# Dividing a top-256 threshold search and its weight subtractions differently between ScalarE, VectorE and GpSimd

## The chip, the cores and the metric

The kernel is one launch on one core of one Trainium2 chip. The core has TensorE (PE) for matrix products, VectorE (DVE), ScalarE (ACT) and GpSimd (POOL) for everything else, and SyncE (SP), which here only starts DMAs. Each engine runs its own list of instructions strictly in order; an instruction whose data or buffer is not there yet holds up everything behind it on its engine. The metric is the time of one execution in device microseconds, lower is better, as the median of three runs.

## The reference, cut to what matters

The reference is one step of a two-layer trunk, for a prompt of 1024 tokens and for eight sample rows of one token each, with a model width of 1024. Layer 0 is a state-space and convolution layer and is not touched. Layer 1 is sparse attention: cheap index scores pick 256 keys for every query, and attention runs over these keys alone.

```python
def index_scores(qi, wi, ki):
    s = jnp.einsum('bthd,bsd->bths', qi, ki, preferred_element_type=jnp.float32) * IDX_DIM ** -0.5
    return jnp.einsum('bths,bth->bts', jax.nn.relu(s), wi.astype(jnp.float32) * IDX_HEADS ** -0.5)

def dsa_attend(q, qi, wi, q_pos, ki_all, gather_kv, topk):
    scores = index_scores(qi, wi, ki_all)
    key_pos = jnp.arange(ki_all.shape[1])
    admissible = key_pos[None, :] <= q_pos[:, None]
    scores = jnp.where(admissible[None], scores, -jnp.inf)
    _, idx = lax.top_k(scores, topk)
    ...
    p = jax.nn.softmax(logits, axis=-1)
    return jnp.einsum('btgrk,btkgd->btgrd', p.astype(v_sel.dtype), v_sel)

def odd_out(x, o, z, w_out, ln_g, ln_b):
    out = (o.reshape(b, l, ATTN_WIDTH) * jax.nn.silu(z)) @ w_out
    return layer_norm(ALPHA * x + out, ln_g, ln_b)
```

Here `q, k, v, qi, ki, wi, z` are slices of one product `x @ w_in`: query, key, value, the three index projections, and the gate.

## The kernel before

The 1024 prompt tokens and the eight sample tokens are one activation of 1032 columns, which layer 1 takes in three chunks of 344 (`CH`). Weights come in tiles of 128 output rows. Each product is made of three matmuls so that it keeps float32 precision: weights and activations are split into a high part, which is the value cast to the matmul's type, and a low part, which is the rest (L131 to L133: high by high, high weight by low activation, low weight by high activation). One weight tile goes through `load_w` and twice through `load_half` (a half is 128x512): a DMA fills `wst`, ScalarE casts it to `whi` (L107), and one engine subtracts to give `wlo` (L108). That engine is VectorE unless the caller passes another. There are three buffers each of `wst`, `whi` and `wlo`.

Layer 1 runs these loops on TensorE: the index projections; the index scores of query blocks 7 to 2 (`SCORE_ROWS`, a block is 128 queries and block tb sees 128(tb+1) keys); eight query tiles (QQ); two key tiles (KK); eight gate tiles (ZZ). Each chunk of a gate tile is evacuated from PSUM by ScalarE (`ev`, L1097). The attention of the eight blocks and the output projection follow. Blocks 0 and 1 have no more than 256 keys and need no search.

The samples' keys are in paged caches. GpSimd starts one indirect DMA per page group (`gather`, L843): 32 of index keys (`in_ckidx`, into an eight-slot buffer that is a tile of pool `q`; L980 multiplies them) and 64 of keys (`in_ck`, eight behind each gate tile, into three buffers; L1077 multiplies them, and a gather of a later tile waits until that has read the buffer).

The 256th largest score of every row is found bit by bit: a round counts the scores at or above a candidate and keeps or drops the candidate's bit. Two methods share the blocks:

- `topk_signs` counts on ScalarE, with the sum of signs (L1137, 32 rounds). Search `a` takes the blocks of `ACT_ROWS` (here 4 and 3: 640 and 512 wide) and search `s` the sample rows (8x1025). After the counts of a round (`jka`, `jks`), VectorE makes three small instructions (L1139, L1121, L1123), and only then can the next round's count start.
- `topk_halves` counts on VectorE. Search `d` takes `DVE_ROWS` (here 7, 6, 5, 2). A copy of each score's upper 16 bits (`UP`, L962) is searched for 16 rounds (`jkd`, L1148). One more count says how many scores are above; then `low` is made of the lower 16 bits (L1164, L1165) in tiles of pool `q`, and searched for 16 more rounds. A row of `bl` costs one count per round.

`masks` turns thresholds into additive masks on VectorE: one count, for `a` and `s` two (L1190), and per block five wide instructions (L1214 to L1218; L1215 is a running sum). The buffers of this stage are closed behind the masks, and the attention's first instruction on VectorE, L1288, which adds the mask to the logits of L1287, stands behind those of `d` and `a`.

The order of the work on each engine is not written in the code: a scheduler places each instruction by its own model of the engines when the program is built. A change in one loop can therefore move instructions of every other.

## Time and profile before

| | |
|---|---|
| runs before | 1779.60, 1783.72 and 1786.36 us, median 1783.72 us |
| the profiled execution | 1771.31 us |
| its span | 1769.5 us |
| mean granted TensorE clock | 0.971 |
| PE busy | 1646.9 us |
| DVE busy | 1076.5 us |
| ACT busy | 782.1 us |
| POOL busy | 495.5 us |
| first count of search `d` | 1037.4 us from the span's start |
| last upper-half count of `d` / last lower-half count | 1184.7 / 1290.2 us |
| first attention instruction on VectorE (L1288) | 1334.51 us |

The profile is of one execution, and instants are counted from its span's start. "Busy" counts an engine's own instructions; a busy engine is not the bound as such. What an engine waited for is inferred from semaphores. TensorE's granted clock is a share of full speed. The stage of the change is from about 990 us, where the first scores are made, to 1334.5 us, where attention begins. The profile gives line numbers of the kernel before; in the kernel after, everything behind L1121 is up to seven lines lower.

### The profile page before, as it was taken

To read this page: it belongs to the slowest core of one execution; us is meant where nothing else is said; L and a number is where in the kernel's file an instruction comes from. 1 tells how busy PE (TensorE), PEld (TensorE's weight loads), DVE (VectorE), ACT (ScalarE), POOL (GpSimd) and SP (SyncE) were. 2 spreads that over 40 slices of the span, in tenths; PEclk is the share of its full clock that TensorE was granted. 3 is DMA by queue.
4 is the path that set the end of the run, shared out by engine and by line. 5 is a ranking of instruction groups with operands and counts; after the bars stand their busy time and mean duration, and the time that the engine had idled before them with its cause. 6 is when DMAs were issued, how large, how long until landed. Compare 5 with 4: busy or idle time off the path is not lost.

```text
span 1769.5 us, 28572 instructions
## 1 busy us (share of the span) xinstructions
PE 1646.9 (93%) x10654; PEld 1467.2 (83%) x10654; DVE 1076.5 (61%) x2632; ACT 782.1 (44%) x1626; POOL 495.5 (28%) x507
## 2 busy tenths in 40 slices
PE   8999999989999999997999999798898997789996
PEld 8999999989999988996898999588795665456674
DVE  4232341551557787757566479799998755355574
ACT  4111111552445554536334355357755653346563
POOL 5242331001212242224224002601555224432120
PEclk9999999999999999998999999899998998899999
DMA  7343343344111264424422213423436333343351
GB/s 241 94 134 109 117 115 96 128 162 170 45 36 56 85 195 149 141 88 131 110 67 87 71 65 102 134 98 110 139 117 196 69 69 102 79 104 81 84 134 47
DMA packets 161836, 192.76 MB, mean 109 GB/s; under 512 B 24144, under 2 KB 122824, under 8 KB 161440
## 3 DMA queue, kind: packets, MB, share of 16 engines
q1 hardware_dynamic: 151920, 166.23, 31.7%
q0 software_dynamic: 8480, 23.31, 4.8%
q8 instruction: 84, 1.38, 0.4%
q10 hardware_dynamic: 1296, 1.38, 0.2%
q14 instruction: 56, 0.46, 0.1%
HBM read 134.73 MB, written 56.14 MB: 108 GB/s over the span
## 4 chain that ended last, share of the span: by engine, by line
PE 76%; DVE 15%; issue 3%; another core or an unknown queue 2%; DMA 2%; ACT 2%; POOL 1%; SPq 0%; DVEq 0%; ACTq 0%; POOLq 0%
PE pp L131 12%; PE pp L133 12%; PE pp L132 12%; PE po L1375 4%; DVE jkd L1148 4%; PE pt L323 4%; PE pv L1323 4%; PE lg L1287 4%; PE tr L1314 3%; PE pt L133 2%; PE pt L132 2%; PE pt L131 2%; PE pt L574 2%; DVE P L1288 1%
## 5 line engine op out<-in xcount | busy, mean ns | idle before, releaser
L131 PE MATMUL pp<-act,whi 128*128 128x344 f32 x1088 | 351.3, 324 | 9.6 <-ACT act L231 8.1
L133 PE MATMUL pp<-act,wlo 128*128 128x344 f32 x1088 | 351.9, 325 | 4.8 <-DVE wlo L108 4.8
L132 PE MATMUL pp<-act,whi 128*128 128x344 f32 x1088 | 351.3, 323 | 0.7 <-POOL act L673 0.6
L131 PEld LDWEIGHTS pp<-act,whi 128*128 128x128 f32 x1088 | 205.5, 189 | 12.2 <-ACT act L231 8.1
L133 PEld LDWEIGHTS pp<-act,wlo 128*128 128x128 f32 x1088 | 205.6, 189 | 6.8 <-DVE wlo L108 5.1
L132 PEld LDWEIGHTS pp<-act,whi 128*128 128x128 f32 x1088 | 205.6, 189 | 3.2 <-issue 1.0
L108 DVE TENSOR_TENSOR wlo<-wst,whi 128x512 fp32r<-128x512 f32 x104 | 72.7, 701 | 161.7 <-ACT whi L107 158.7
L107 ACT CAST whi<-wst 128x512 fp32r<-128x512 f32 x148 | 91.0, 618 | 173.2 <-PE pp L132 58.7
L131 PE MATMUL pp<-yh,whi 128*128 128x344 f32 x408 | 135.1, 331 | 9.0 <-issue 5.0
L133 PE MATMUL pp<-yh,wlo 128*128 128x344 f32 x408 | 133.9, 328 | 6.4 <-issue 3.7
L318 POOL TENSOR_TENSOR cft<-cw,own 128x640 f32<-128x640 f32 x64 | 86.0, 1379 | 165.8 <-PE pt L323 154.7
L1288 DVE CUSTOM_DVE_ANT_0 P<-lg,w 128x512 f32<-128x512 f32 (+3 forms) x144 | 83.1, 597 | 81.0 <-PE lg L1287 41.4
L1287 PE MATMUL lg<-w,Q 128*128 128x512 f32 (+3 forms) x384 | 107.9, 385 | 13.7 <-DVE nmx L1288 13.5
L843 POOL DMA_INDIRECT q<-in_ck,idx x64 | 68.4, 1069 | 117.3 <-PE pt L1077 83.5
L108 POOL TENSOR_TENSOR wlo<-wst,whi 128x512 fp32r<-128x512 f32 x44 | 58.1, 1324 | 150.6 <-ACT whi L107 130.5
L1314 PE MATMUL tr<-cst,P 128*128 128x128 f32 x576 | 89.1, 287 | 5.4 <-issue 3.9
L1287 PEld LDWEIGHTS lg<-w,Q 128*128 128x128 f32 x384 | 65.2, 198 | 34.5 <-DVE nmx L1288 21.8
L1314 PEld LDWEIGHTS tr<-cst,P 128*128 128x128 f32 x576 | 67.0, 145 | 32.2 <-issue 23.4
L1292 ACT ACTIVATE P<-P,mx 128x1024 f32<-128x1024 f32 (+3 forms) x64 | 63.3, 989 | 68.6 <-DVE mx L1291 56.6
L1323 PE MATMUL pv<-ph,V 128*64 128x256 f32 (+1 forms) x640 | 85.2, 381 | 8.9 <-ACT ph L1319 4.2
L131 PEld LDWEIGHTS pp<-yh,whi 128*128 128x128 f32 x408 | 78.4, 192 | 17.9 <-issue 11.0
L133 PEld LDWEIGHTS pp<-yh,wlo 128*128 128x128 f32 x408 | 78.3, 192 | 9.1 <-issue 4.9
(568 smaller groups left out, 4028.7 us busy)
## 6 DMA issues: line engine op xcount, KB each, us to landing
wst<-in_W SPq DMA_DIRECT2D x148, 256.0 KB
Q<-dq SPq DMA_DIRECT2D x64, 256.0 KB
dq<-ev SPq DMA_DIRECT2D x48, 172.0 KB
xst<-in_xT SPq DMA_DIRECT2D x8, 516.0 KB
dzb<-ob SPq DMA_DIRECT2D x24, 172.0 KB
uv<-dzb SPq DMA_DIRECT2D x8, 516.0 KB
dza<-ob SPq DMA_DIRECT2D x24, 172.0 KB
dyb<-uv SPq DMA_DIRECT2D x8, 516.0 KB
```

The costliest lines, as they stand in the source:

```text
L107: nc.scalar.copy(hi, st)
L108: (eng or nc.vector).tensor_tensor(lo, st, hi.bitcast(F32), op=ALU.subtract)
L131: nc.tensor.matmul(out, wh, ah, start=(start and kt == 0), stop=False)
L132: nc.tensor.matmul(out, wh, al, start=False, stop=False)
L133: nc.tensor.matmul(out, wl, ah, start=False, stop=(stop and kt == 7))
L318: nc.gpsimd.tensor_tensor(wt.rearrange("q d (c p) -> q d c p", p=PH), cw[:, g, : NBT - 1].rearrange("q (d p) -> q d p", p=PH).unsqueeze(2) ...
L323: nc.tensor.matmul(p[:, j, :], wt[:, d, :], up[:, g, 4 - d : 4 - d + BL], start=(d == 0), stop=(d == NSH - 1))
L1148: nc.vector.tensor_scalar(jk, col, c, 0.0, op0=op, op1=ALU.add, accum_out=cnt)
L1287: mm = nc.tensor.matmul(lg, Q[:, 4 * a + r, :], KT[g][:, s0 : s0 + m], start=(a == 0), stop=(a == 1))
L1288: nc.vector.tensor_tensor_reduce(out=P[:, s0 : s0 + m], in0=lg, in1=M[tb][:, s0 : s0 + m], scale=-0.125, scalar=BIG, op0=ALU.add, op1=ALU. ...
L1314: nc.tensor.transpose(p[:, a, r * 128 : r * 128 + 128], Ps[r][:, (sb + a) * 128 : (sb + a) * 128 + 128], k.ident)
L1323: nc.tensor.matmul(pv[64 * u : 64 * u + 64, 256 * pr + c0 : 256 * pr + c1], V[:, sb + a, g * 64 : g * 64 + 64], ph[:, a, c0:c1], start=(sb ...
```

## The change

Three things are changed, all in layer 1.

1. `SCORE_ROWS` is now 7, 6, 5, 4, 3, 2. Block 2 moves from search `d` (VectorE) to search `a` (ScalarE). A round of `a` now has three counts, one of `d` three in place of four. The `UP` copies stand behind block 5's scores.
2. The query, key and gate weights are loaded with `eng=nc.gpsimd`: 18 tiles, 36 subtractions L108 go from VectorE to GpSimd.
3. In search `d`, the update of the candidate for bits 30 to 16 is one instruction in place of two. The comparison yields 0 or the bit in its place, and one instruction flips that bit and sets the next one to be tried.

```diff
-SCORE_ROWS = (7, 6, 5, 2, 3, 4)
-ACT_ROWS = (4, 3)
-DVE_ROWS = (7, 6, 5, 2)
+SCORE_ROWS = (7, 6, 5, 4, 3, 2)
+ACT_ROWS = (4, 3, 2)
+DVE_ROWS = (7, 6, 5)
...
-        w = load_w(k, A["W"][QQ + i])
+        w = load_w(k, A["W"][QQ + i], eng=nc.gpsimd)
...
-        w = load_w(k, A["W"][KK + i])
+        w = load_w(k, A["W"][KK + i], eng=nc.gpsimd)
...
-        w = load_w(k, A["W"][ZZ + i])
+        w = load_w(k, A["W"][ZZ + i], eng=nc.gpsimd)
...
-    def search(name, R_, cols, count, above, last):
+    def search(name, R_, cols, count, above, last, placed=False):
...
-            above(no, cnt)
+            above(no, cnt, bit)
             new = k.t(tk, [R_, n], U32, "cand" + name, 2)
-            if bit == 31:
-
-                nc.vector.tensor_scalar(new.bitcast(I32), no, -1.0, None, op0=ALU.mult)
+            flip = 1 << (bit - 1) if bit > last else 0
+            if bit < 31 and placed:
+                nc.vector.scalar_tensor_tensor(new, no, flip, cand, op0=ALU.bitwise_xor, op1=ALU.bitwise_xor)
             else:
-                nc.vector.scalar_tensor_tensor(new, no, bit, cand, op0=ALU.logical_shift_left, op1=ALU.bitwise_xor)
-            if bit > last:
-                nc.vector.tensor_scalar(new, new, 1 << (bit - 1), None, op0=ALU.bitwise_xor)
+                if bit == 31:
+
+                    nc.vector.tensor_scalar(new.bitcast(I32), no, -1.0, None, op0=ALU.mult)
+                else:
+                    nc.vector.scalar_tensor_tensor(new, no, bit, cand, op0=ALU.logical_shift_left, op1=ALU.bitwise_xor)
+                if flip:
+                    nc.vector.tensor_scalar(new, new, flip, None, op0=ALU.bitwise_xor)
             cand = new
         return cand
...
-        cand = search(name, 128, UP, count, lambda no, cnt: nc.vector.tensor_scalar(no, cnt, float(TOPK), None, op0=ALU.is_lt), 16)
+        def above(no, cnt, bit):
+            nc.vector.tensor_scalar(no, cnt, float(TOPK), float(1 << bit) if bit < 31 else 1.0, op0=ALU.is_lt, op1=ALU.mult)
+
+        cand = search(name, 128, UP, count, above, 16, placed=True)
```

With other engines and other lengths, the scheduler orders the stage anew. Three places show it. In the rows, a line, an operation, and the tile written `<-` those read are given.

The first place is VectorE between the last counts of search `d`'s upper halves (`jkd` from `topd`) and its lower halves (`q<-S`, L1164). `noa`, `canda` are search `a`, `nos` is search `s`. Before:

```order
L1148 TENSOR_SCALAR jkd_12875,k2d_12870<-w_9633,topd_12868 128x896
L1161 TENSOR_SCALAR sgnd_12871<-sgnd_12871 128x4
L1139 TENSOR_TENSOR noa_12445<-cnta_12444,lima_12319 128x2
L1148 TENSOR_SCALAR jkd_12877,k2d_12870<-w_9634,topd_12868 128x768
L1164 TENSOR_SCALAR q_12885<-S_9635,sgnd_12871,offd_12872 128x1024
L1164 TENSOR_SCALAR q_12885<-S_9635,sgnd_12871,offd_12872 128x896
L1121 SCALAR_TENSOR_TENSOR canda_12451<-noa_12445,canda_12441 128x2
L1164 TENSOR_SCALAR q_12886<-S_9635,sgnd_12871,offd_12872 128x768
```

And now (L1171 is the lower half, L1143, L1125 and L1127 are a round's three small instructions):

```order
L1152 TENSOR_SCALAR jkd_12895,k2d_12888<-w_9634,topd_12886 128x768
L1143 TENSOR_TENSOR noa_12409<-cnta_12408,lima_12318 128x3
L1164 TENSOR_SCALAR k2d_12888<-k2d_12888 128x3
L1125 SCALAR_TENSOR_TENSOR canda_12417<-noa_12409,canda_12405 128x3
L1127 TENSOR_SCALAR canda_12417<-canda_12417 128x3
...
L1143 TENSOR_TENSOR noa_12445<-cnta_12444,lima_12318 128x3
L1125 SCALAR_TENSOR_TENSOR canda_12453<-noa_12445,canda_12441 128x3
L1127 TENSOR_SCALAR canda_12453<-canda_12453 128x3
L1171 TENSOR_SCALAR q_12901<-S_9635,sgnd_12889,offd_12890 128x1024
L1171 TENSOR_SCALAR q_12901<-S_9635,sgnd_12889,offd_12890 128x896
```

In place of one round of search `a`, four stand in a row ahead of the lower halves (the two left out at "..." read like those shown), and the subtractions `wlo` are gone from there.

The second place is ScalarE at the end of the search, around the last counts of `a` (`jka`) and the evacuations of the gate tiles (`ev`). Before:

```order
L1097 ACTIVATE ev_11988<-pp_11963 128x344
L1137 ACTIVATE jks_13355,cnts_13353<-Ss_9636,cands_13350 8x1025
L1137 ACTIVATE jka_12636,cnta_12634<-S_9635,canda_12631 128x640
L1137 ACTIVATE jka_12638,cnta_12634<-S_9635,canda_12631 128x512
L1097 ACTIVATE ev_12016<-pt_11991 128x344
L1137 ACTIVATE jks_13363,cnts_13361<-Ss_9636,cands_13358 8x1025
L107 CAST whi_12079<-wst_12077 128x512
L107 CAST whi_12193<-wst_12191 128x512
L1097 ACTIVATE ev_12044<-pp_12019 128x344
L1137 ACTIVATE jks_13371,cnts_13369<-Ss_9636,cands_13366 8x1025
L1097 ACTIVATE ev_12108<-pt_12083 128x344
L1137 ACTIVATE jks_13379,cnts_13377<-Ss_9636,cands_13374 8x1025
```

And now, at the last two rounds of `a`:

```order
L1141 ACTIVATE jka_12678,cnta_12672<-S_9635,canda_12669 128x384
L1141 ACTIVATE jka_12686,cnta_12684<-S_9635,canda_12681 128x640
L1141 ACTIVATE jka_12688,cnta_12684<-S_9635,canda_12681 128x512
L1097 ACTIVATE ev_12135<-pp_12110 128x344
L1141 ACTIVATE jka_12690,cnta_12684<-S_9635,canda_12681 128x384
L107 CAST whi_12198<-wst_12196 128x512
L1141 ACTIVATE jka_12698,cnta_12696<-S_9635,canda_12693 128x640
L1141 ACTIVATE jka_12700,cnta_12696<-S_9635,canda_12693 128x512
L1097 ACTIVATE ev_12163<-pt_12138 128x344
L1141 ACTIVATE jka_12702,cnta_12696<-S_9635,canda_12693 128x384
L1101 COPY ki_11337<-pt_10237 128x512
L1097 ACTIVATE ev_12227<-pp_12202 128x344
```

Before, the last count of `a` had eight of the gate stage's 24 evacuations behind it, and counts of `s` between them; now it has three behind it, and one evacuation stands inside each of its last rounds.

The third place is GpSimd in the gate tiles. Before, only the gathers of `in_ck` stood there, eight for a tile. Now, around one tile's subtractions:

```order
L843 DMA q_11340<-in_ck,idx_8869 128x256
L108 TENSOR_TENSOR wlo_11719<-wst_11716,whi_11718 128x512
L843 DMA q_11339<-in_ck,idx_8869 128x256
...
L843 DMA q_11340<-in_ck,idx_8869 128x256
L108 TENSOR_TENSOR wlo_11833<-wst_11830,whi_11832 128x512
L843 DMA q_11339<-in_ck,idx_8869 128x256
...
L843 DMA q_11339<-in_ck,idx_8869 128x256
L108 TENSOR_TENSOR wlo_11839<-wst_11836,whi_11838 128x512
L843 DMA q_11338<-in_ck,idx_8869 128x256
```

Each gate tile now has two subtractions among its eight gathers, on the same engine and in order with them; up to four gathers stand between the two.

More of the change, by code (lines that the diff above doesn't have):

```diff
@@ L1137, in count @@
             nc.scalar.activation(jk, s, AF.Sign, bias=c, scale=-1.0, accum_out=cnt)
-        return search(name, R_, bl, count, lambda no, cnt: nc.vector.tensor_tensor(no, cnt, lim, op=ALU.is_gt), 0)
+        return search(name, R_, bl, count, lambda no, cnt, bit: nc.vector.tensor_tensor(no, cnt, lim, op=ALU.is_gt), 0)
     def topk_halves(name, bl):
```

## The prediction

> **What bounds the kernel now.** I read the page first, for the engines and the chain that ended last.
>
> ```profile
> PE 1646.9 (93%) x10654; PEld 1467.2 (83%) x10654; DVE 1076.5 (61%) x2632; ACT 782.1 (44%) x1626; POOL 495.5 (28%) x507
> PE 76%; DVE 15%; issue 3%; another core or an unknown queue 2%; DMA 2%; ACT 2%; POOL 1%; SPq 0%; DVEq 0%; ACTq 0%; POOLq 0%
> ```
>
> TensorE is busy nearly throughout and carries three quarters of the chain; VectorE carries 15%. So a change on the other engines counts only where the chain leaves TensorE. The second view, the windows (stretch, its length, then busy time and instructions of PE, PEld, DVE, ACT, POOL, granted clock, DMA share, GB/s), finds that place.
>
> ```profile
> 1100.00:1150.00 50.00, 39.62 (x202) 31.00 (x202) 40.25 (x119) 18.18 (x43) 31.59 (x33) 0.86 0.49 138
> 1150.00:1200.00 50.00, 47.63 (x277) 41.50 (x276) 49.21 (x151) 28.93 (x68) 3.81 (x4) 1.00 0.32 107
> 1200.00:1250.00 50.00, 42.84 (x293) 38.95 (x292) 49.03 (x164) 36.32 (x79) 16.14 (x16) 0.97 0.38 116
> 1250.00:1300.00 50.00, 43.60 (x332) 40.86 (x332) 49.42 (x173) 37.11 (x80) 22.80 (x23) 0.97 0.40 124
> ```
>
> From 1150 to 1300 VectorE is busy 49 of every 50 us, TensorE 134.1 of 150. ScalarE and GpSimd have room: 102.4 and 42.8 of 150. VectorE is the full queue of this stage. What ends the stage stands in the chain of waits from 1250 on (start, length, engine, tile, line), of which these pieces are the last before attention.
>
> ```profile
> 1320.90 0.89 DVE eq L1190 x2
> 1333.30 1.28 DVE eq L1190 x2
> 1334.58 0.60 DVE P L1288
> ```
>
> The masks of search `a` run from 1320.9 to 1333.3 (12.4 us), after those of `d`, and one count of `s` follows; then L1288 starts attention. That alone would make VectorE's chain the bound. The timeline shows the other clock.
>
> ```profile
> 1298.87 0.73 ACT L1137 ACTIVATE jka<-S,canda 128x512 bf16<-128x512 f32 x1
> 1318.46 0.43 ACT L1097 ACTIVATE ev<-pt 128x344 f32<-128x344 f32 x1
> 1320.42 1.15 ACT L1137 ACTIVATE jks<-Ss,cands 8x1025 bf16<-8x1025 f32 x1 [0.79 <-DVE cands L1123]
> 1329.23 0.46 ACT L1097 ACTIVATE ev<-pp 128x344 f32<-128x344 f32 x1 [3.37 <-PE pp L133]
> ```
>
> ```profile
> 1330.08 1.20 PE L1287 MATMUL lg<-w,Q 128*128 128x512 f32 x4
> 1335.24 3.24 PE L1287 MATMUL lg<-w,Q 128*128 128x512 f32 x6 [3.96 <-DVE nmx L1288]
> ```
>
> The last count of `a` (first row) ended at 1299.6, 21 us before its masks could start: ScalarE was early, VectorE late. But TensorE's last gate chunk was evacuated at 1329.2 (fourth row), and its first logits stood at 1331. TensorE waited 4 us for the masks and no more. **Both chains end within 4 us of each other**, so a shorter VectorE queue is worth at most those 4 us unless TensorE's gate tiles end earlier too.
>
> **The change part by part.** All sums are for the instant of L1288, 1334.5 in the profiled execution (1771.31 us, 0.7% below the median of the runs, 1783.72; I add the difference to the median).
>
> What leaves VectorE ahead of the end of `d`'s masks (groups from 1036 to 1335: busy us, mean ns, idle before):
>
> ```profile
> L108 DVE TENSOR_TENSOR wlo<-wst,whi 128x512 fp32r<-128x512 f32 x33 | 22.5, 683 | 2.8 <-issue 2.4 <-DMA dz<-ev 0.4
> L1148 DVE TENSOR_SCALAR_CACHE_REDUCE jkd<-w,candd 128x384 bf16<-128x384 bf16 x16 | 9.7, 607 | 0.1
> L1148 DVE TENSOR_SCALAR_CACHE_REDUCE jkd<-q,testd 128x384 bf16<-128x384 uint16 x16 | 9.6, 602 | 0.0
> L1123 DVE TENSOR_SCALAR candd<-candd 128x4 uint32<-128x4 uint32 x15 | 2.7, 178 | 0.3
> L1139 DVE TENSOR_TENSOR noa<-cnta,lima 128x2 uint32<-128x2 f32 x32 | 4.8, 149 | 0.0
> ```
>
> ```profile
> 1290.82 0.68 DVE L108 TENSOR_TENSOR wlo<-wst,whi 128x512 fp32r<-128x512 f32 x1
> 1291.42 0.17 DVE L1173 TENSOR_TENSOR ged<-cntd,k2d 128x4 f32<-128x4 f32 x1
> 1318.21 0.96 DVE L1215 TENSOR_TENSOR_SCAN cum<-eq 128x384 f32<-128x384 f32 x1
> 1319.20 0.62 DVE L1216 SCALAR_TENSOR_TENSOR eq<-cum,needd,eq 128x384 f32<-128x384 f32 x1
> ```
>
> Block 2 costs 16 counts of 607 ns and 16 of 602: 19.3 us. One more count in the search and one in the masks are 1.2, its five wide mask instructions, two of which are shown, about 3 (an estimate from these two), its copy and low halves about 1: together 24. A subtraction holds the queue for 0.60 us, as the start of the next instruction shows; 33 of them are 20. The 15 second bit updates of 178 ns, each 0.15 by start to start, are 2.3. Sum: 46 us, on a queue that is full; it comes off nearly whole.
>
> What leaves the stretch without leaving the path: when the masks of `d` are done, eight rounds of `a` and eleven of `s` are still to come in the new order (before, almost none). Their 57 small instructions, of up to 0.15 us each, are 8.5 us, of which I take 6, since in a full queue starts stand closer than durations (0.60 against 0.68 above). They go to the tail.
>
> What is added: four rounds of `a` stand in a row ahead of the lower halves, with nothing between them to do, so VectorE waits there for ScalarE three times. ScalarE's durations:
>
> ```profile
> L1137 ACT ACTIVATE jks<-Ss,cands 8x1025 bf16<-8x1025 f32 x32 | 36.8, 1150 | 24.8 <-DVE cands L1123 13.2 <-issue 6.6 <-DVE canda L1121 4.5
> L1137 ACT ACTIVATE jka<-S,canda 128x640 bf16<-128x640 f32 x32 | 26.3, 822 | 25.9 <-DVE canda L1123 17.2 <-DVE nos L1139 4.7 <-DVE jkd L1148 2.5
> L1137 ACT ACTIVATE jka<-S,canda 128x512 bf16<-128x512 f32 x32 | 23.0, 718 | 0.4
> L107 ACT CAST whi<-wst 128x512 fp32r<-128x512 f32 x33 | 19.9, 609 | 3.6 <-PE pt L980 2.9 <-PE pp L132 0.5
> L1097 ACT ACTIVATE ev<-pt 128x344 f32<-128x344 f32 x12 | 5.3, 446 | 8.9 <-PE pt L133 3.3 <-PE pp L133 3.3 <-remote 2.3
> ```
>
> A count of 384 is estimated at 0.61 us, on the line through 512 (718 ns) and 640 (822). A round of `a` is then 2.15 us on ScalarE, and about 0.8 for VectorE's three instructions and the way back: the row of `jks` at 1320.42 above shows 0.79 idle on `cands`. Three rounds of 2.95, less the instructions already counted, are 8 us. It is nothing if ScalarE ran ahead, and 12 if casts and evacuations stand between; I take 8.
>
> The subtractions on GpSimd cost VectorE something too where both read their operands at once. No row shows L108 of GpSimd against a score row of VectorE; the nearest pair is from layer 0:
>
> ```profile
> 669.55 0.51 DVE L658 TENSOR_TENSOR gz<-gz,gz 128x344 f32<-128x344 f32 x1
> 670.45 2.52 DVE L658 TENSOR_TENSOR gz<-gz,gz 128x344 f32<-128x344 f32 x1
> 670.22 2.37 POOL L673 TENSOR_TENSOR act<-big,act 128x1032 fp32r<-128x1032 f32 x1 [7.00 <-ACT act L672]
> ```
>
> The same subtraction-like instruction took 0.51 us alone and 2.52 us beside GpSimd's, and ended 0.4 us after it. Of VectorE's instructions with two full operands the score updates are the main ones, and they lie with the query subtractions. If ten of the 36 meet one and hold it for half of GpSimd's 1.32 us (row below), VectorE loses 6 us, part of it in slack; I take 3. Ends: 0, and 24 if all 36 meet one. The Trainium skill, "SBUF — State Buffer", section "Who interferes with whom", says that a VectorE instruction with two SBUF inputs and a GpSimd instruction that reads SBUF exclude each other for a whole instruction, and that one with at most one SBUF input is free. By this rule of the Trainium skill each of the ten could be held for all of GpSimd's 1.32 us, 13 us in place of 3, and the sum would be 1796. The layer 0 pair agrees with it (2.52 us against 0.51).
>
> So `d`'s masks end at 1320.9 - 46 - 6 + 8 + 3 = 1280.
>
> The **tail** is now ScalarE's: 8 rounds of 2.15, 11 of 1.15, and by its new order 12 evacuations of 0.44 and 7 casts of 0.61 among them: 17.2 + 12.7 + 5.3 + 4.3 = 39.5. The last five rounds of `a` have no round of `s` to fill their 0.8 us way through VectorE: 4 more. `a` ends at 1280 + 43.5 = 1323.5. Its masks then take 12.4 and 1.2 for two counts of block 2 (the rest of block 2 stands behind L1288): 1337, or **2.5 us later** than before.
>
> A second gate says the same: the last count of `a` stands behind all but three evacuations. That one started at 1318.46. With TensorE where it was, 1318.5 + 0.4 + 0.6 + 0.8 + 13.6 = 1334. Whatever VectorE saves, attention cannot start earlier unless TensorE does.
>
> Does TensorE? In a gate tile it is GpSimd that now has ten instructions (PE and POOL rows of the timeline, the group of L108, a wait):
>
> ```profile
> 1317.77 0.32 PE L132 MATMUL pp<-yb,whi 128*128 128x344 f32 x1
> 1317.93 0.32 PE L133 MATMUL pp<-yh,wlo 128*128 128x344 f32 x1
> L108 POOL TENSOR_TENSOR wlo<-wst,whi 128x512 fp32r<-128x512 f32 x44 | 58.1, 1324 | 150.6 <-ACT whi L107 130.5
> 1128.25 0.95 POOL L843 DMA_INDIRECT q<-in_ck,idx  x1 [0.30 <-issue]
> 1129.51 0.96 POOL L843 DMA_INDIRECT q<-in_ck,idx  x1 [0.30 <-issue]
> 1329.07 1.08 PE L1077 MATMUL pt<-q,q 128*32 128x128 f32 x32
> POOL q L843 <- PE pt L1077: 83.5, 8, 34.9
> ```
>
> TensorE starts a matmul each 0.16 us: a tile of 72 with 32 small ones (1.08) is 12.6 us. GpSimd's eight gathers at 1.26 from start to start and two subtractions at 1.32 are 12.7, no slack. Before, a late gather cost little; now a subtraction of the next tile stands behind it, and TensorE's `wlo` with it. On the other side TensorE no longer waits for VectorE's `wlo`. I bound the gate stage by 15 us earlier (the gaps of 1150 to 1300) and 16 later (eight tiles with a 2 us landing each, an estimate from the idle between gathers), and take nothing.
>
> Behind the start, five instructions of block 2 (3 us) stand between VectorE's first logits:
>
> ```profile
> 1334.50:1500.00 165.50, 148.07 (x915) 100.26 (x917) 110.93 (x309) 87.88 (x152) 62.13 (x57) 0.92 0.43 109
> ```
>
> VectorE has a third of this stage free, which hides them; uncovered, they cost 3 us. Nothing else behind 1334.5 changes.
>
> The sum is +2.5 us on 1771.3, so 1773.8; with the median, **1786 us**.
>
> **The rivals.**
>
> *Faster (1768 us).* The 10 us in which TensorE crawled in 1100 to 1150 (39.62 busy, clock 0.86) lie where GpSimd started gathers back to back; its new subtractions spread them. With these, and with no `wlo` waiting behind wide counts, the gate tiles end some 15 us earlier, and VectorE, 10 us of whose idle time lies in that window too, ends `d` near 1268: `a` ends at 1311, attention starts near 1320 to 1325, 10 to 15 us earlier. Taking 15: 1768. For it: VectorE's full queue, and the 21 us that `a` waited. Against: ScalarE's tail is unchanged by all this.
>
> *Slower (1799 us).* ScalarE and TensorE lock. A round of `a` has an evacuation inside it, which waits for a chunk; the chunk waits for `wlo`; that stands on GpSimd behind gathers that wait for L1077 of a tile before. It decides once GpSimd's 12.7 us, plus waits, pass TensorE's 12.6; 2 us a tile over eight tiles are 16 us, less the 3 us that the tail has over the second gate: +13 to +16, 1799. For it: the sum of a tile, and 83.5 us that GpSimd waited for L1077 before. Against: those waits were slack, with gathers alone behind them.
>
> *The exclusion on the operands decides.* With 24 us instead of 3 on VectorE: attention 21 us later, 1807. The counts (most of VectorE's time) have one full operand, which speaks against it.
>
> **How the numbers follow.** 0.5%, 9 us, is what a measurement here can tell from no change. The forecast (within about 9 us of before) gets 0.44; faster 0.33; slower by the lock 0.17, by the operands 0.06. The likeliest case alone spans 1775 to 1793. The range reaches into both sides: 1766 to 1802, with about a tenth left out at each end. So faster 0.33, same 0.44, slower 0.23.
>
> **What would show it.** Right: `d`'s masks end near 1280, VectorE idle for some 8 us ahead of L1171, then mostly idle until `a` ends near 1320; L1295 (the old L1288) first at 1330 to 1340. The share of VectorE in 1150 to 1300 falls from 49 of 50 below 40. A step is wrong if `a` ends before 1312 (the tail was too dear), if TensorE waits for GpSimd's `wlo` by more than 10 us in the gate tiles (the lock), or if the score updates L952 get much longer (the operands). The prediction fails as a whole if TensorE's gate tiles end more than 10 us away from 1330.

## The result, and the profile after

The kernel after takes 1798.69 us (median of five runs, 1795.58 to 1799.99) against 1783.72 before: a ratio of 1.0103, 95% interval 1.0069 to 1.0137. It is 15 us slower, where 1786 us, no change, was forecast. The profiled execution's span is 1796.9 us, 27.4 more than that of before, at a mean granted clock of 0.960 (before 0.971); the profiled execution of before was a quick one, 12.4 us under its median, so the traces below show a larger loss than the medians do. Attention's first instruction on VectorE (L1295) stands at 1359.39 us in place of 1334.51, so 24.9 of the 27.4 us are made ahead of it. The kernel before took about 1730 us in some calls of the experiments below and 1778 to 1784 in others, for a reason that no run shows, so ratios are always to the kernel before in the same call.

The page first: busy time by engine, and the shares of the chain that ended last.

```profile
PE 1659.9 (92%) x10654; PEld 1481.5 (82%) x10654; DVE 1057.3 (59%) x2516; ACT 802.4 (45%) x1690; POOL 540.4 (30%) x543
PE 76%; DVE 11%; issue 5%; ACT 2%; DMA 2%; POOL 1%; another core or an unknown queue 0%; ACTq 0%; SPq 0%; DVEq 0%; POOLq 0%
```

VectorE does 19 us less, ScalarE 20 and GpSimd 45 more, as the change says. TensorE does the same 10654 matmuls in 13 us more busy time. The windows (columns as in the prediction) say when:

```profile
1100.00:1150.00 50.00, 41.08 (x216) 32.84 (x216) 42.82 (x116) 20.96 (x53) 35.59 (x37) 0.93 0.48 134
1150.00:1200.00 50.00, 35.83 (x175) 32.32 (x175) 36.76 (x101) 29.37 (x71) 12.02 (x12) 0.76 0.27 82
1200.00:1250.00 50.00, 41.62 (x259) 39.37 (x257) 48.71 (x143) 34.35 (x78) 9.56 (x8) 0.90 0.24 78
1250.00:1300.00 50.00, 40.05 (x301) 37.59 (x302) 46.13 (x118) 32.51 (x73) 36.63 (x30) 0.90 0.41 124
```

From 1150 to 1200 TensorE is busy 35.83 us where it was 47.63, at a clock of 0.76 where it was 1.00. Over the four windows its busy time falls from 173.7 to 158.6 us, 15 less, and the clock that was withheld, 50 x (1 - clock) summed, rises from 10.0 to 25.5 us: two losses that cannot simply be added, since in these windows the clock is lowest where TensorE is busy least. The evacuations of the query tiles show that the loss begins there, ahead of the gate tiles (a summary of ScalarE's L1025 over 1140 to 1210, before and then after: count, durations, first and last start):

```profile
L1025 ACT CAST ev<-pp x9: 418/425/448, 1143.4 to 1189.1; 128x344 fp32r<-128x344 f32 x9
```

```profile
L1025 ACT CAST ev<-pp x9: 418/427/446, 1139.9 to 1205.4; 128x344 fp32r<-128x344 f32 x9
```

These are the last nine of 24 chunks in both. The last query chunk comes 16.3 us late. At the last gate chunk (1329.23 before) it is 25.2:

```profile
1354.17 0.17 PE pp L133
1354.41 0.46 ACT ev L1097
```

These are from the chain of waits of after. What happens between is in the timelines of VectorE, of ScalarE and of TensorE, around the place where four rounds of `a` now stand in a row:

```profile
1172.24 0.16 DVE L1143 TENSOR_TENSOR noa<-cnta,lima 128x3 uint32<-128x3 f32 x1 [2.64 <-ACT jka L1141]
1175.43 0.16 DVE L1143 TENSOR_TENSOR noa<-cnta,lima 128x3 uint32<-128x3 f32 x1 [2.63 <-ACT jka L1141]
1178.63 0.16 DVE L1143 TENSOR_TENSOR noa<-cnta,lima 128x3 uint32<-128x3 f32 x1 [2.63 <-ACT jka L1141]
1178.83 0.16 DVE L1125 SCALAR_TENSOR_TENSOR canda<-noa,canda 128x3 uint32<-128x3 uint32 x1
1178.96 0.52 DVE L1026 TENSOR_TENSOR ev<-pp,ev 128x344 fp32r<-128x344 f32 x1
```

```profile
1177.89 0.61 ACT L1141 ACTIVATE jka<-S,canda 128x384 bf16<-128x384 f32 x1
1178.51 0.42 ACT L1025 CAST ev<-pp 128x344 fp32r<-128x344 f32 x1
```

```profile
1171.50 0.43 PE L980 MATMUL pt<-q,q 128*64 128x128 f32 x2
1179.53 0.66 PE L131 MATMUL pp<-yh,whi 128*128 128x344 f32 x1 [7.61 <-DVE ev L1026]
1179.99 0.49 PE L132 MATMUL pp<-yb,whi 128*128 128x344 f32 x1
1180.27 0.49 PE L133 MATMUL pp<-yh,wlo 128*128 128x344 f32 x1
```

VectorE waits three times 2.6 us, the 8 us of the prediction. But behind the rounds stands a query chunk's evacuation: its high part on ScalarE (L1025) behind the last count, its low part on VectorE (L1026) behind the last wait. There are two buffers `pp`; both are full, and TensorE stops for 7.61 us. Then its matmuls start 0.29 us apart for some 5 us, where the gate tiles of before had 0.16: a stop is paid twice. From 1145 to 1152 TensorE also crawls, with starts 1.4 us apart:

```profile
1147.67 0.32 PE L133 MATMUL pp<-yh,wlo 128*128 128x344 f32 x1 [1.07 <-issue]
```

Before has the like from about 1129 to 1142 (the slow stretch that the prediction saw), so this is not what sets the two apart.

### The profile page after: what moved, and what is told of

It is laid out like the page before. It is cut to its first block, busy times and chain, and to the rows that moved or that the text cites. A ratio compares the mean times of both kernels' runs of the same rounds, so it can differ in the third digit from the quotient of the medians.

```text
span 1796.9 us, 28561 instructions
## 1 busy us (share of the span) xinstructions
PE 1659.9 (92%) x10654; PEld 1481.5 (82%) x10654; DVE 1057.3 (59%) x2516; ACT 802.4 (45%) x1690; POOL 540.4 (30%) x543
## 4 chain that ended last, share of the span: by engine, by line
PE 76%; DVE 11%; issue 5%; ACT 2%; DMA 2%; POOL 1%; another core or an unknown queue 0%; ACTq 0%; SPq 0%; DVEq 0%; POOLq 0%
PE pp L131 12%; PE pp L133 12%; PE pp L132 12%; PE po L1382 4%; PE pt L323 4%; PE pv L1330 3%; PE tr L1321 3%; PE lg L1294 3%; DVE jkd L1152 3%; PE pt L131 2%; PE pt L132 2%; PE pt L133 2%; PE pt L574 2%; PE pt L548 1%; DVE P L1295 1%
## 5 line engine op out<-in xcount | busy, mean ns | idle before, releaser
L108 POOL TENSOR_TENSOR wlo<-wst,whi 128x512 fp32r<-128x512 f32 x80 | 105.9, 1326 | 324.3 <-ACT whi L107 302.3
L108 DVE TENSOR_TENSOR wlo<-wst,whi 128x512 fp32r<-128x512 f32 x68 | 47.2, 697 | 157.2 <-ACT whi L107 157.0
L1295 DVE CUSTOM_DVE_ANT_0 P<-lg,w 128x512 f32<-128x512 f32 (+3 forms) x144 | 83.1, 596 | 75.7 <-PE lg L1294 38.9
L1141 ACT ACTIVATE jka<-S,canda 128x640 bf16<-128x640 f32 (+2 forms) x96 | 68.9, 718 | 33.9 <-DVE canda L1127 14.2
```

The costliest lines, as they stand in the source:

```text
L108: (eng or nc.vector).tensor_tensor(lo, st, hi.bitcast(F32), op=ALU.subtract)
L1295: nc.vector.tensor_tensor_reduce(out=P[:, s0 : s0 + m], in0=lg, in1=M[tb][:, s0 : s0 + m], scale=-0.125, scalar=BIG, op0=ALU.add, op1=ALU. ...
```

## The experiments

Ratios are to the kernel before in the same call, with their 95% intervals.

| run | edit | before, us | ratio |
|---|---|---|---|
| wlo_only | part 2 alone | 1730 | 1.0181 [1.0152, 1.0209] |
| rows_bits | parts 1 and 3 | 1730 | 1.0021 [1.0005, 1.0038] |
| query_on_vector | change, query tiles on VectorE | 1730 | 1.0087 [1.0061, 1.0113] |
| bits_only | part 3 alone | 1730 | 0.9968 [0.9950, 0.9986] |
| after_again | the change | 1778 | 1.0123 [1.0091, 1.0155] |
| after_spread | change, rounds of `a` spread | 1778 | 1.0160 [1.0133, 1.0188] |
| wlo_spread | wlo_only, rounds of `a` spread | 1778 | 1.0156 [1.0127, 1.0184] |
| before_spread | before, rounds of `a` spread | 1778 | 1.0022 [0.9995, 1.0048] |
| after_order | change, order of rows_bits | 1730 | 1.0082 [1.0061, 1.0103] |
| wlo_order | wlo_only, order of before | 1730 | 1.0108 [1.0080, 1.0136] |
| qq_order | query_on_vector, order of rows_bits | 1730 | 1.0084 [1.0057, 1.0111] |
| no_gather_vector | rows_bits, no gathers | 1779 | 0.9956 [0.9923, 0.9990] |
| no_gather_gpsimd | change, no gathers | 1779 | 1.0033 [0.9999, 1.0066] |
| bits_q4 | part 3, four query tiles on GpSimd | 1779 | 1.0046 [1.0009, 1.0084] |
| nogather_vector_2 | as above | 1731 | 0.9995 [0.9985, 1.0004] |
| nogather_gpsimd_2 | as above | 1731 | 1.0072 [1.0056, 1.0088] |
| nogather_twice | nogather_vector_2, idle subtractions on GpSimd | 1731 | 1.0052 [1.0035, 1.0069] |
| bits_only_2 | part 3 alone | 1731 | 0.9972 [0.9960, 0.9984] |

**Which part.** The parts are taken apart by leaving `eng=nc.gpsimd` out or `ROWS` as before:

```diff
-        w = load_w(k, A["W"][QQ + i], eng=nc.gpsimd)
+        w = load_w(k, A["W"][QQ + i])
```

> The kernel before with the second part alone: the low parts of query, key and gate weights on GpSimd, rows and bit updates as before. Theory of the parked rounds (VectorE waits for four rounds of search a ahead of the lower halves, and the query evacuations behind them hold TensorE): that wait is not in this order, so no loss of 20 us; 1770 to 1792 us, first L1288 at 1320 to 1340. Theory of the lock (GpSimd's gathers and subtractions hold the gate tiles): the loss is here already, 1793 us or more, TensorE waiting for wlo in the gate tiles.

> The change without its second part: block 2 on ScalarE and the short bit updates, all subtractions on VectorE. Parked rounds: no round of a stands alone ahead of the lower halves here, so no stop of 8 us there; 1775 to 1792. Theory of ScalarE's tail (three counts a round and eight rounds behind the masks of d set the end): slower as the whole change is, 1793 to 1802, with TensorE's gate tiles ending on time and waiting for the masks.

> The changed kernel, with the subtractions of the eight query tiles back on VectorE; key and gate stay on GpSimd. The four rounds of a are no longer ahead of the lower halves in this order. Parked rounds: attention starts 15 to 25 us earlier than in the changed kernel, 1775 to 1788. Lock: the gate tiles are as in the changed kernel, so 1793 to 1800. Tail: 1793 to 1802.

> The kernel before with the shorter bit updates alone: 15 VectorE instructions less, 2.3 us of a full queue. All theories: within 0.3% of before, 1778 to 1788, because TensorE's gate tiles end within 4 us of the masks; if VectorE's queue alone set the end, 2 us faster.

The subtractions are the loss: alone they cost 1.8%, and without them the other parts are within 0.5%. Part 3 alone gains 0.3%. Two of the four did not come out as the parked rounds would have it. wlo_only was expected to have none and lost most; TensorE waits there 1.1 us in all for GpSimd's `wlo`, so it is not the lock either. query_on_vector, with no four rounds in a row, still loses 0.9%: the order cannot be all. In wlo_only TensorE's waits for query evacuations (from 990 to 1340; us, times, longest) and the ScalarE timeline at the longest, abridged, read:

```profile
PE pp L131 <- DVE ev L1026: 26.2, 4, 13.6
```

```profile
1143.61 0.83 ACT L1137 ACTIVATE jka<-S,canda 128x640 bf16<-128x640 f32 x1 [2.87 <-DVE canda L1123]
...
1148.94 0.83 ACT L1137 ACTIVATE jka<-S,canda 128x640 bf16<-128x640 f32 x1 [3.56 <-DVE canda L1123]
...
1153.77 0.83 ACT L1137 ACTIVATE jka<-S,canda 128x640 bf16<-128x640 f32 x1 [3.06 <-DVE canda L1123]
...
1155.44 0.43 ACT L1025 CAST ev<-pp 128x344 fp32r<-128x344 f32 x1
```

Three rounds of `a`, some 5 us apart because each waits for VectorE's `canda` behind a round of `d`, stand ahead of one evacuation. That is the mechanism of after, with the rows unmoved: in after VectorE waits for ScalarE's counts, here ScalarE for VectorE's, and in both an evacuation stands behind. Taking part 2 away removes it: no stop above 2.5 us is left in rows_bits.

**The order.** If the order alone makes the loss, spreading the rounds of `a` by hand should end it; in after_spread each is bound behind one more query evacuation:

```diff
-            for j, col in enumerate(cols):
-                count(col, cand.bitcast(F32)[:, j : j + 1], cnt[:, j : j + 1])
+            gate_a = name == "a"
+            with tc.issue_after(EVQ[min(23, 11 + 31 - bit)]) if gate_a else ExitStack():
+                for j, col in enumerate(cols):
+                    count(col, cand.bitcast(F32)[:, j : j + 1], cnt[:, j : j + 1])
```

> The changed kernel itself, for the chip of this call. By the first measurement 1.0103 of before; both theories: 1.006 to 1.016.

> The changed kernel, with each round of search a made to issue on ScalarE no earlier than the next query evacuation (the first behind the twelfth, then one more a round): same instructions on the same engines, another order. In the changed kernel four rounds (12 counts) stand between two query evacuations; here never more than two. Order theory (rounds of a, paced by trips between ScalarE and VectorE, stand ahead of the evacuation that TensorE's two PSUM buffers wait for): TensorE's longest stop in the query tiles falls from 7.9 us to under 4, attention starts 12 to 22 us earlier than in the changed kernel, 0.996 to 1.004 of before. Theory of the engine's work (GpSimd delivers the low parts late, whatever the order): within 5 us of the changed kernel, 1.007 to 1.014.

> The kernel with the GpSimd subtractions alone, which gave 1.0181 of before, with the same rule for the rounds of a. Order theory: the stop of 13.8 us in the query tiles goes, 15 to 20 us faster, 1.004 to 1.010 of before. Engine's work: 1.014 to 1.020.

> The kernel before with the same rule for the rounds of a, as a control: its order already has no more than two rounds between query evacuations. Order theory: 0.996 to 1.004. If the rule itself, and not the stop, makes the time: as much faster as the two kernels above become.

The control before_spread stays where it was (1.0022), but the two spread kernels are no faster, against the theory of the order: wlo_spread lies where the other theory put it, and after_spread above both ranges. The trace says why: the rule held rounds of `a` back on ScalarE, and the scheduler put whole rounds of `d` ahead of the low part on VectorE instead. TensorE in wlo_spread:

```profile
1163.96 0.65 PE L131 MATMUL pp<-yh,whi 128*128 128x344 f32 x1 [14.04 <-DVE ev L1027]
```

So every count of `a`, `s` and `d` was bound behind as many casts and evacuations as stand ahead of it in the kernel with VectorE's subtractions (`GT` holds the pairs):

```diff
-            nc.scalar.activation(jk, s, AF.Sign, bias=c, scale=-1.0, accum_out=cnt)
+            with behind(name):
+                nc.scalar.activation(jk, s, AF.Sign, bias=c, scale=-1.0, accum_out=cnt)
```

> The changed kernel, with every count of the three searches made to issue behind as many casts (whi) and evacuations of the query, key and gate tiles as stand ahead of it in the kernel rows_bits (ScalarE: casts and evacuations; VectorE: low parts of evacuations). So the order of rounds against the work that TensorE waits for is that of rows_bits (1.0021 of before), and only the engine of the 36 subtractions differs. Order theory: 0.998 to 1.006 of before, no stop of TensorE over 4 us from 1100 to 1200. Theory of the engine's work (GpSimd's subtractions are late, or their exclusion with VectorE costs): 1.009 to 1.018, TensorE waiting for wlo.

> The kernel with the GpSimd subtractions alone (1.0181 of before, and 1.0156 with the rounds of a spread), with all counts placed against casts and evacuations as in the kernel before. Order theory: 0.996 to 1.005, and the stops of 6 and 14 us in the query tiles go. Engine's work: 1.012 to 1.019.

> The kernel query_on_vector (key and gate subtractions on GpSimd, 1.0087 of before), with the counts placed as in rows_bits. Order theory: 0.998 to 1.005, and the stop of 7 us for a cast at the change of gate tiles goes. Engine's work: 1.006 to 1.012.

wlo_order and after_order lie between the ranges of the two theories, so neither explains them alone; qq_order lies in the range of the engine's work and is no faster than query_on_vector (1.0084 and 1.0087). wlo_order is the clean reading: 1.0181 becomes 1.0108, each beside a before of 1730 us, so the order is 0.7% of the 1.8%. For the whole change the figure is not sure: it ran unbound only in calls with a before of 1778 us or more (1.0103 and 1.0123), after_order (1.0082) in one of 1730, and one kernel's ratio can differ by 0.4% between the two (no_gather_vector below has 0.9956 in the one and, as nogather_vector_2, 0.9995 in the other). About 0.8 to 1.1% stays with the order restored, where no single wait of TensorE is above 5.2 us. In wlo_order the largest sums, up to 1340, are:

```profile
PE pt L132 <- ACT whi L107: 8.2, 3, 4.5
PE pt L1080 <- DMA q<-in_ck,idx: 8.0, 4, 5.2
PE pp L134 <- POOL wlo L109: 5.3, 3, 4.1
```

**The gathers.** The second and third row could be GpSimd's queue, where gathers and subtractions hold one another: my rival of the lock. Without gathers there is no such queue. These kernels read fixed rows with plain DMAs, so they leave out the collection of the samples' pages; in no_gather_gpsimd the counts are bound to the order of no_gather_vector:

```diff
-        nc.gpsimd.indirect_dma_start(out=dst, out_offset=None, in_=src,
-                                     in_offset=bass.IndirectOffsetOnAxis(ap=idx[:, j : j + 1], axis=0))
+        if src is A["ck"] or src is A["ckidx"]:
+            b = 128 * (j % 64 if j < 64 else j - 64)
+            nc.sync.dma_start(dst, src[b : b + 128])
...
```

> Block 2 on search a and the shorter bit updates, subtractions on VectorE (as rows_bits), but the 96 indirect DMAs of GpSimd that collect the samples' index keys and keys are plain DMAs of SyncE from fixed rows: it leaves out the collection of the samples' cache pages. The control of the next run. Against the kernel before I expect 0.985 to 1.005 under both theories. Attention's first instruction on VectorE some 0 to 10 us earlier than in rows_bits (1316.5).

> The whole change, with the same plain DMAs in place of GpSimd's gathers and the search counts bound to the order of no_gather_vector. GpSimd's queue then holds the subtractions alone. If the 0.8% that stayed in after_order is made by gathers and subtractions that hold one another in GpSimd's queue, this ends within 0.3% of no_gather_vector, and attention starts within 5 us of it. If it is the exclusion on the operands, or the 1.33 us that a subtraction takes on GpSimd against 0.68 on VectorE, it ends 0.6% or more behind no_gather_vector, with attention 10 us or more later.

> The shorter bit updates alone (bits_only), and the subtractions of the first four query tiles on GpSimd; the other fourteen tiles' stay on VectorE. These lie before the parked rounds of search a. If subtractions on GpSimd cost by the order of the evacuations and by the queue of late gathers, this is 0.994 to 0.999 of the kernel before, as bits_only (0.9968); if they cost something each wherever they stand (0.8% over 36 is 0.02% each), it is 0.998 to 1.000. If the built order parks rounds ahead of the query evacuations here too, 1.005 or more.

The difference of the pair is 0.8% (1.0033 / 0.9956), not under 0.3%: the lock is not needed. Attention starts 7.6 us later (1329.8 for 1322.2), less than the 10 expected. bits_q4 lies between its ranges, 0.8% above what part 3 gave alone, with no stop of TensorE above 3.1 us; but bits_only ran only in calls with a before of 1730 us, so what four tiles cost by themselves stays open.

**The operands.** What is left is the exclusion on the operands or the longer way of a tile, 1.3 us on GpSimd for 0.68. nogather_twice has the first without the second: VectorE keeps `wlo`, and GpSimd subtracts for nobody; the counts are bound as in the run before it.

```diff
+    if twice is not None:
+        du = k.t(k.wpool, [128, 256], BF16, "wdu", 1)
+        for c in (0, 256):
+            nc.gpsimd.tensor_tensor(du, twice[:, c : c + 256], hi.bitcast(F32)[:, c : c + 256], op=ALU.subtract)
```

> no_gather_vector again, as the control beside the two next runs on the same chip. No theory sets it apart; about 0.99 to 1.00 of the kernel before.

> no_gather_gpsimd again beside its control, since the difference of the two (0.7%) was not far outside their intervals. If subtractions on GpSimd cost without any gather, 0.4 to 1.0% behind nogather_vector_2; if the first pair was chance, within 0.3%.

> no_gather_vector, VectorE keeps its subtractions, and GpSimd makes, right behind each cast, subtractions of the same two-operand kind (two of 128x256 for each of the 36 halves) from a stored activation and the cast weight, whose result nothing uses. Counts are bound to the order of no_gather_vector. It leaves out the collection of the samples' cache pages, as its control. VectorE's small instructions meet GpSimd's operands as in the change, but no matmul waits for GpSimd. If the exclusion on the operands makes the loss, this is 0.4 to 1.0% behind nogather_vector_2, and VectorE's small two-operand instructions (noa, nos, kept) are longer as in no_gather_gpsimd. If the loss is made by the longer way of a weight tile (1.33 us on GpSimd in place of 0.68), it is within 0.3% of nogather_vector_2 though the small instructions are longer.

> The shorter bit updates alone (bits_only) on this chip, beside bits_q4, which missed. If the four query tiles on GpSimd made bits_q4 slow, 0.993 to 1.000 of the kernel before, as the first time (0.9968); if the shorter updates themselves do not help on this chip, 1.002 or more.

nogather_twice is 0.6% behind its control (1.0052 / 0.9995), nogather_gpsimd_2 0.8%. The groups of VectorE's instructions from 990 to 1320 (busy us, mean ns, idle before), first of the control, then of nogather_twice:

```profile
L108 DVE TENSOR_TENSOR wlo<-wst,whi 128x512 fp32r<-128x512 f32 x41 | 28.0, 685 | 9.7 <-ACT whi L107 9.7
L1129 DVE SCALAR_TENSOR_TENSOR canda<-noa,canda 128x3 uint32<-128x3 uint32 x29 | 4.5, 154 | 0.3
L1147 DVE TENSOR_TENSOR nos<-cnts,lims 8x1 uint32<-8x1 f32 x32 | 4.6, 143 | 7.4 <-ACT jks L1145 7.3
L1156 DVE TENSOR_SCALAR_CACHE_REDUCE jkd<-w,candd 128x1024 bf16<-128x1024 bf16 x16 | 20.4, 1275 | 0.1
```

```profile
L109 DVE TENSOR_TENSOR wlo<-wst,whi 128x512 fp32r<-128x512 f32 x41 | 31.1, 760 | 9.7 <-ACT whi L107 9.7
L1151 DVE SCALAR_TENSOR_TENSOR canda<-noa,canda 128x3 uint32<-128x3 uint32 x25 | 5.9, 236 | 0.2
L1170 DVE TENSOR_TENSOR nos<-cnts,lims 8x1 uint32<-8x1 f32 x32 | 6.2, 193 | 5.0 <-ACT jks L1168 4.9
L1180 DVE TENSOR_SCALAR_CACHE_REDUCE jkd<-w,candd 128x1024 bf16<-128x1024 bf16 x16 | 20.4, 1274 | 0.1
```

Instructions with two operands in SBUF are longer, down to eight partitions of one element (143 to 193 ns); the counts, with one full operand, are not (1275 and 1274). The means come from single meetings: 17 small instructions of the searches take over 0.4 us in nogather_twice, none in the control, and each of the 17 ends within 0.03 us of the end of one of GpSimd's subtractions. Three of them have one operand only (`nod`, and `canda` made of `canda` alone), so two operands are not needed for it. ScalarE's casts wait for GpSimd 0.4 us in all, so the idle subtractions do not act by holding `whi`. VectorE is full here (busy 49 of every 50 us from 1100 to 1250 in both), so it passes the loss on: attention starts at 1335.0 in place of 1322.7, and the span is 13.5 us longer (1742.8 against 1729.3). So **the exclusion alone is enough for a loss of this size** (0.6% by the medians). Two reservations: in the change VectorE also gets some 26 us of subtractions off its queue, which nogather_twice doesn't have; and GpSimd's idle subtractions took 63.8 us there against 50.2 in nogather_gpsimd_2. In the latter only 3.3 us are lost by the start of attention (1326.0), and 6.6 more between the first and the 65th logits (129.8 us for 123.2). There `mx`, of two operands of 128x1, is longer; control, then nogather_gpsimd_2:

```profile
L1302 DVE TENSOR_TENSOR mx<-nmx 128x1 f32<-128x1 f32 x32 | 10.1, 316 | 0.2
```

```profile
L1322 DVE TENSOR_TENSOR mx<-nmx 128x1 f32<-128x1 f32 x32 | 15.5, 483 | 0.2
```

That is 5.4 us in a stage where GpSimd has other work: five `mx` are over 0.4 us in the control and eight in nogather_gpsimd_2, and each ends within 0.02 us of the end of another two-operand instruction of GpSimd (`wl`, `yo` and the like). I read it as the same exclusion on other instructions; that it makes all of the 6.6 us wasn't tried by itself.

That bits_only_2 repeats 0.997 makes part 3 alone the best version measured, ahead of before by 0.3% and, by the ratios, of the change by over 1%.

**Why the rows gain nothing.** By the medians of one call, rows_bits is 9.4 us slower than bits_only (1734.2 against 1724.9). Their two profiled executions lie closer: attention starts 11.6 us earlier in rows_bits (1316.5 against 1328.1), and the span is 0.8 us longer (1728.3 against 1727.5). But the early start is in part apparent: in rows_bits search `a` ends only at 1328.0, and its masks follow between attention's instructions, where in bits_only they were made ahead of it. The windows from the 33rd to the 65th logits, rows_bits and then bits_only:

```profile
1370.70:1439.70 69.00, 63.30 (x417) 43.07 (x414) 52.69 (x130) 41.66 (x71) 33.22 (x25) 1.00 0.39 100
```

```profile
1381.30:1438.70 57.40, 56.75 (x395) 41.00 (x396) 36.29 (x107) 31.39 (x58) 15.52 (x17) 1.00 0.28 65
```

Work that had been ahead of attention stands in this stage now. `mx` rows of the same windows, by groups of VectorE:

```profile
L1298 DVE TENSOR_TENSOR mx<-nmx 128x1 f32<-128x1 f32 x17 | 9.5, 557 | 0.1
```

```profile
L1298 DVE TENSOR_TENSOR mx<-nmx 128x1 f32<-128x1 f32 x16 | 3.7, 229 | 0.4
```

GpSimd is busy 33.22 us in place of 15.52, and `mx` takes 557 ns in place of 229. I see the 11.6 us come back here; which part is `mx` and which the masks of the sample rows, which fell into the same window, was not tried apart, and the medians' 9.4 us are more than these two executions can show.

## Why the prediction was wrong, point by point

- **Both chains end together ahead of attention.** Right, and it held: L1295 starts at 1359.39, when the masks of `a` end, 4.5 us after the last gate evacuation.
- **VectorE waits 8 us ahead of L1171.** Right: 2.64 + 2.63 + 2.63 = 7.9.
- **`d`'s masks end at 1280.** They ended at 1295.9. VectorE's idle time from 1036 to that end (1320.9 before) rose by 9 us (18.4 to 27.5), near the 8 that were forecast; its busy time fell by 34 (266.5 to 232.4), where the sum has 46 + 6 - 3 = 49. So what came out too small is busy time, and I took 3 us of it for the operands, between 0 and 24. By the groups of VectorE from 1000 to attention, seven two-operand rows (`noa`, `nos`, `canda`, `cands`, `keptd` and two of the score updates) grew by 16 us together. The trace shows the meetings: 13 small instructions of the searches took over 0.4 us, 15.5 us together (before: none), and each ended within 0.03 us of the end of one of GpSimd's subtractions, such as this one:

```profile
1286.14 1.25 DVE L1143 TENSOR_TENSOR noa<-cnta,lima 128x3 uint32<-128x3 f32 x1
1285.82 1.55 POOL L108 TENSOR_TENSOR wlo<-wst,whi 128x512 fp32r<-128x512 f32 x1
```

  Eleven of the 13 lie ahead of 1295.9. Three of the rows before, to which `noa` comes with the 149 ns of the prediction's row:

```profile
L1139 DVE TENSOR_TENSOR nos<-cnts,lims 8x1 uint32<-8x1 f32 x32 | 4.6, 143 | 0.8 <-issue 0.6
L1175 DVE SCALAR_TENSOR_TENSOR keptd<-ged,keptd 128x4 f32<-128x4 f32 x16 | 2.5, 159 | 0.1
L952 DVE SCALAR_TENSOR_TENSOR S<-cum,wi,S 128x384 f32<-128x384 f32 x8 | 4.9, 615 | 0.3
```

And after:

```profile
L1143 DVE TENSOR_TENSOR noa<-cnta,lima 128x3 uint32<-128x3 f32 x32 | 9.6, 299 | 23.6 <-ACT jka L1141 19.3 <-issue 4.0
L1143 DVE TENSOR_TENSOR nos<-cnts,lims 8x1 uint32<-8x1 f32 x32 | 9.4, 295 | 21.5 <-ACT jks L1141 12.6 <-issue 8.9
L1182 DVE SCALAR_TENSOR_TENSOR keptd<-ged,keptd 128x3 f32<-128x3 f32 x16 | 3.7, 230 | 0.0
L952 DVE SCALAR_TENSOR_TENSOR S<-cum,wi,S 128x384 f32<-128x384 f32 x8 | 6.1, 761 | 0.6 <-ACT cum L948 0.6
```

  I had counted on ten of the 36 subtractions to meet a wide score update, for half of one each. The small instructions of the search, some 170 of which have two operands (32 each of `noa` and `nos`, 31 each of `canda` and `cands`, 16 or 15 each of `ged`, `keptd` and `candd`), were not in the count, though each can be held by GpSimd just as long. The Trainium skill, "SBUF — State Buffer", section "Who interferes with whom", makes no exception for size: the pair excludes one another for a whole instruction. These rows agree with it in kind. The prediction's sentence on the page leaves out a condition: by the same section of the Trainium skill, an instruction with at most one SBUF input is free only outside VectorE's two-port modes. One of the 13 has one input (`canda` from `canda`, 1.25 us); which mode it ran in, no trace here shows.
- **The tail, 43.5 us from `d` to `a`.** It was 49.8 (1295.9 to 1345.7), of the right kind and 6 us too short: ScalarE waited 4.9 us inside it for TensorE's late chunks. The masks of `a`, 13.6 us, took 13.7.
- **TensorE: "take nothing".** This is the step that failed, beside the 3 us for the operands. I bounded only the gate tiles, by GpSimd's gathers, and took the query and key tiles as they were, though the first order block showed four rounds moved together. I priced the three waits for VectorE's queue, and did not ask what else stands behind them on both engines: a query evacuation, of which TensorE has two chunks' worth of buffers. Of the 25.2 us by which the gate tiles end late, 16.3 are there at the last query chunk. The prediction's own second gate then gives the time: the evacuation with three behind it started at 1344.3 in place of 1318.5, and 1344.3 + 0.4 + 0.6 + 0.8 + 13.6 is 1359.7, where attention started at 1359.4. The prediction had named gate tiles more than 10 us away from 1330 as what would make it fail.
- **The lock.** Its time, 1799, is what came, by luck and not by its mechanism: only 9 of the 25 us fall in the key and gate tiles, where TensorE's longest waits are for a cast (5.4 us), a key tile's low part on VectorE (4.8) and a gather (3.9). No wait of TensorE for GpSimd's `wlo` is seen, where over 10 us was the sign, and the loss against a control survives without any gather.
- **The faster rival.** It hoped that spread gathers would end TensorE's crawl. The crawl came later and stayed.
- **The gain of VectorE, 46 us less.** VectorE's busy time fell by 19 us only (1076.5 to 1057.3): the operands took back some 16, some 4 us of block 2's masks were only moved, and these rows do not account for the rest. Its share from 1150 to 1300 is 43.9 of every 50 us, where below 40 was forecast. It bought nothing, for by the second gate above TensorE came later.

What stays open: how the 15 us of the medians divide between the order and the operands. The order is shown by wlo_only against wlo_order, the operands by nogather_twice; on the change itself the two were not separated in one call. Single executions of different calls give a rough division at the last gate evacuation: it starts at 1329.2 before, 1315.9 in rows_bits, 1333.6 in after_order (the subtractions on GpSimd in rows_bits' order) and 1354.4 in after. By these the rows and bits gained 13 us there, the subtractions cost 18 and the order 21 more; the no-gather kernels, which ran in calls of both speeds, differ there by up to 4.4 us from call to call.

## What to carry to other kernels

When a change makes one queue shorter, look at where the scheduler parks the work that was between: a serial search's rounds put ahead of an evacuation stop TensorE for the whole of the rounds, once the few PSUM buffers are full. Moving a two-operand instruction from VectorE to GpSimd is not free for VectorE even when the two never depend on each other: look through every instruction that VectorE runs beside it, the small ones first, since there are the most of them. And a term that is bounded for one stage (the gate tiles) must be bounded for each stage in which the moved instructions stand.

## What the runs showed of the hardware

Two groups of small instructions with two SBUF operands, `noa` (128x3) and `nos` (8x1), doubled on average beside GpSimd's 1.3 us subtractions. A summary of the 32 `noa` of after (shortest, median and longest in ns, first and last start) shows how:

```profile
L1143 DVE TENSOR_TENSOR noa<-cnta,lima x32: 139/156/1967, 1113.2 to 1345.3; 128x3 uint32<-128x3 f32 x32
```

The median, 156 ns, is near the mean of before (149); three meetings, of 1.25, 1.76 and 1.97 us, make the new mean. The longest ones are longer than the subtraction they end with (1.27 to 1.29 us): GpSimd was starting a gather just ahead of it. Stops of TensorE of 3.8 and 7.6 us were followed by matmuls 0.29 us apart in place of 0.16 for 4 to 5 us, as at 1179.53 above.
